# Joining the 32-wide inverse blocks of both head groups in one run on eight 32x32 tiles, with VectorE's block transpose for the transposed block

## The chip, the cores and the metric

The kernel runs on one core of one Trainium2 chip, as one program. Time is the device time of one launch in microseconds, and a kernel's time is the median of its runs. TensorE's matmuls, VectorE (DVE in the profile), ScalarE (ACT), GpSimd (POOL) and the DMA queues run side by side, each engine through its own list of instructions in order, and wait for each other by semaphores.

## The reference

A trunk of two layers over 256 tokens of width 1024. Each layer computes a gated DeltaNet branch in both directions and a differential attention branch from one input projection, gates and merges them, and projects out. The part that matters here is the DeltaNet's chunked form: in every chunk and head, and in both directions, a unit triangular matrix is inverted.

```python
    decay = jnp.where(lower, jnp.exp(jnp.where(lower, gdiff, 0.0)), 0.0)
    L = jnp.where(strict, jnp.einsum('bhncd,bhnmd->bhncm', kb, k) * decay, 0.0)
    eye = jnp.eye(CHUNK, dtype=f32)
    T = lax.linalg.triangular_solve(eye + L, jnp.broadcast_to(eye, L.shape),
                                    left_side=True, lower=True, unit_diagonal=True)
    u = jnp.einsum('bhncm,bhnme->bhnce', T, vb)
    w = jnp.einsum('bhncm,bhnmd->bhncd', T, kb * jnp.exp(g)[..., None])
```

Around it stand the large projections, `proj = h @ w_in[l]` (1024 x 10272), `y_a @ w_pa[l]`, `y_b @ w_pb[l]` and `merged @ w_out[l]`.

## The kernel before

**Projections.** Every projection of 512 columns is a stream of 128x512 products on TensorE. A weight block `kp` (256 rows, two of the eight `kt`) comes in by DMA as `raw`; ScalarE rounds it to `hi` (line 308), VectorE takes the rest as `lo` (line 310), and TensorE adds three products for each token tile `m`: input high by `hi` (line 324), input high by `lo` (line 325), input low by `hi` (line 326). So a block costs twelve 128x512 products, and those of line 325 can't start before VectorE has made `lo`. Buffers for `hi` and `lo` are two each. `gb` and `ga` are the two gate projections, each in two halves; the numbers in a name such as `lo_ga002` are layer, half and `kp`.

**The inverse.** Chunks of 128 tokens are used, two (`c`) for each of eight heads and two directions (`d`). Heads go in two groups `g` of four (`j4`). VectorE inverts the 32x32 diagonal blocks by substitution earlier in the layer. Then TensorE joins the blocks: 32 wide to 64 wide in `merges(g)`, 64 wide to 128 wide in `join()`, and `chunks(g)` uses the result. `U_` (`U` for a group) holds the inverses at 128 columns for each of 16 cases, `T64` the blocks in the other orientation at 64 columns, `A` the decayed products of the keys. To join two 32-blocks b0 and b1, the kernel makes

- `y64p` = A(b0, b1) by T64(b0), which ScalarE copies to `y64` (lines 926 and 930);
- `zt64` from `y64` and U(b1); ScalarE writes it negated as the off-diagonal block of `U` (lines 940 and 952);
- `z64`, the same block in the other orientation and for the pair `mm == d` alone; ScalarE writes it negated into `T64` (lines 945 and 955).

`srcdst(d, mm)` gives (0, 1) or (2, 3) for direction 0, and (1, 0) or (3, 2) for direction 1. An operand's 32-partition quarter sets the row of TensorE's 32x32 tile that a product uses, and the quarter of its result in PSUM sets the column. So a group's products stand on four tiles in `y64p` and `zt64` and on two in `z64`. `T64` and `U` then go into `y128p` and `zt128` of `join()` (line 966), 64x64 products of both groups on four 64x64 tiles, whose results ScalarE evicts (lines 973, 975 and 983).

**What sets the order.** The program is scheduled ahead of the run, and then fixed on every engine. `behind(x)` makes an instruction stand after instruction x; `place(n)` is the last product of the n-th `kt` in the list of projections `zb, za, gb, ga, pb` (eight `kt` a half, so 32 to 47 is `gb` and 48 to 63 is `ga`). `run(gen, at)` issues one step of a generator behind `place(at)`; the list `order` near line 1267 says which step goes where. `weigh_q` (line 830) multiplies a PSUM bank of key-query products `kq` (line 789) by the decays on VectorE. `gate_yb` has VectorE scale the attention output (line 1202) and turn it in 32x32 blocks (line 249); it is issued in the same stretch.

## Time and profile before

| | before |
|---|---|
| median of 3 runs | 747.26 us (746.84 to 748.62) |
| profiled execution, its own time | 746.91 us |
| its span, first to last instruction | 745.2 us |
| TensorE matmul busy | 736.4 us (99%) |
| VectorE, ScalarE, GpSimd busy | 585.9 (79%), 482.5 (65%), 141.8 us (19%) |
| mean granted TensorE clock | 0.999 |

The profile is of one execution. In its timeline a row gives a start in us from the span's start, the time until the last instruction of the row has ended, the engine, line, operation, output<-inputs, the tile of TensorE, the shape and a count; in brackets stands how long the engine had been idle before it, and what it had waited for. An fp32 product on TensorE shows as two matmul instructions, an fp32r one (the projections) as one. The end of a matmul is modelled, so the step between two starts says more than a duration.

### The profile page before, as it was taken

To read this page: it belongs to the slowest core of one execution; us is meant where nothing else is said; L and a number is where in the kernel's file an instruction comes from. 1 tells how busy PE (TensorE), PEld (TensorE's weight loads), DVE (VectorE), ACT (ScalarE), POOL (GpSimd) and SP (SyncE) were. 2 spreads that over 40 slices of the span, in tenths; PEclk is the share of its full clock that TensorE was granted. 3 is DMA by queue.
4 is the path that set the end of the run, shared out by engine and by line. 5 is a ranking of instruction groups with operands and counts; after the bars stand their busy time and mean duration, and the time that the engine had idled before them with its cause. 6 is when DMAs were issued, how large, how long until landed. Compare 5 with 4: busy or idle time off the path is not lost.

```text
span 745.2 us, 13923 instructions
## 1 busy us (share of the span) xinstructions
PE 736.4 (99%) x5176; PEld 638.4 (86%) x5176; DVE 585.9 (79%) x1109; ACT 482.5 (65%) x1024; POOL 141.8 (19%) x221
## 2 busy tenths in 40 slices
PE   9999999999999999999999999999999999999996
PEld 6999899987888889888889899889778888998885
DVE  8696898999986865578668779899999769638782
ACT  6757775567877586645456578565787758666552
POOL 6004111112022442100000150202110425301000
PEclk9999999999999999999999999999999999999999
DMA  8755566776766462567674466768666737336641
GB/s 260 240 171 171 169 172 195 216 204 205 209 182 173 148 193 89 171 203 241 204 233 130 131 194 177 214 175 237 200 170 198 199 120 233 106 119 203 216 142 58
DMA packets 73734, 135.46 MB, mean 182 GB/s; under 512 B 12944, under 2 KB 13921, under 8 KB 73666
## 3 DMA queue, kind: packets, MB, share of 16 engines
q1 hardware_dynamic: 64750, 113.65, 50.7%
q0 software_dynamic: 7936, 19.35, 9.1%
q10 hardware_dynamic: 980, 1.58, 0.6%
q8 instruction: 41, 0.67, 0.4%
q14 instruction: 27, 0.22, 0.1%
HBM read 125.53 MB, written 9.01 MB: 181 GB/s over the span
## 4 chain that ended last, share of the span: by engine, by line
PE 96%; ACT 2%; issue 1%; DVE 1%; POOLq 0%; POOL 0%; DVEq 0%; ACTq 0%
PE pp_vb L369 4%; PE pp_qk L325 4%; PE pp_qk L326 3%; PE pp_qk L324 3%; PE sc L1072 2%; PE pp_o L369 2%; PE pf_k L385 2%; PE pp_za L325 2%; PE pf_v L385 2%; PE pf_v L389 2%; PE pp_gb L325 2%; PE pp_gb L324 2%; PE pp_zb L324 2%; PE pf_q L387 2%; PE pf_k L387 2%; PE pf_v L387 2%
## 5 line engine op out<-in xcount | busy, mean ns | idle before, releaser
L325 PE MATMUL pp_qk<-lo_qk,hT 128*128 128x512 f32 x128 | 50.5, 395 | 0.3 <-DVE lo_qk L310 0.2
L326 PE MATMUL pp_qk<-hi_qk,hT 128*128 128x512 f32 x128 | 49.9, 390 | 0.0
L310 DVE TENSOR_TENSOR lo_qk<-raw_qk,hi_qk 128x1024 fp32r<-128x1024 f32 x32 | 39.0, 1220 | 9.8 <-ACT hi_qk L308 9.5
L324 PE MATMUL pp_qk<-hi_qk,hT 128*128 128x512 f32 x128 | 45.1, 393 | 0.0
L308 ACT CAST hi_qk<-raw_qk 128x1024 fp32r<-128x1024 f32 x28 | 29.4, 1050 | 23.4 <-PE pp_qk L326 12.7
L1082 ACT ACTIVATE es<-sc,mx 128x256 f32<-128x256 f32 x64 | 29.7, 475 | 19.6 <-DVE mx L1080 19.6
L310 DVE TENSOR_TENSOR lo_pb<-raw_pb,hi_pb 128x1024 fp32r<-128x1024 f32 x16 | 19.6, 1224 | 25.2 <-ACT hi_pb L308 25.2
L387 PE MATMUL pf_q<-hT,hi_q 128*128 128x256 f32 x128 | 36.1, 286 | 0.0
L385 PE MATMUL pf_k<-hT,hi_k 128*128 128x256 f32 x128 | 36.0, 287 | 0.0
L385 PE MATMUL pf_v<-hT,hi_v 128*128 128x256 f32 x128 | 35.9, 285 | 0.0
L387 PE MATMUL pf_v<-hT,hi_v 128*128 128x256 f32 x128 | 35.8, 284 | 0.0
L387 PE MATMUL pf_k<-hT,hi_k 128*128 128x256 f32 x128 | 35.7, 284 | 0.0
L385 PE MATMUL pf_q<-hT,hi_q 128*128 128x256 f32 x128 | 35.7, 284 | 0.0
L389 PE MATMUL pf_q<-hT,lo_q 128*128 128x256 f32 x128 | 35.2, 288 | 0.0
L389 PE MATMUL pf_v<-hT,lo_v 128*128 128x256 f32 x128 | 34.5, 288 | 0.0
L389 PE MATMUL pf_k<-hT,lo_k 128*128 128x256 f32 x128 | 34.3, 283 | 0.0
L308 ACT CAST hi_pa<-raw_pa 128x1024 fp32r<-128x1024 f32 x16 | 16.9, 1055 | 22.2 <-PE pp_pa L326 16.1
L679 DVE SCALAR_TENSOR_TENSOR cvq<-pf_q,cw,cvq 128x254 f32<-128x254 f32 (+1 forms) x64 | 29.9, 477 | 0.9 <-ACT cvq L675 0.2
L679 DVE SCALAR_TENSOR_TENSOR cvk<-pf_k,cw,cvk 128x254 f32<-128x254 f32 (+1 forms) x64 | 29.0, 477 | 1.4 <-ACT cvk L675 0.6
L325 PEld LDWEIGHTS pp_qk<-lo_qk,hT 128*128 128x128 f32 x128 | 24.0, 188 | 6.7 <-DVE lo_qk L310 1.7
L679 DVE SCALAR_TENSOR_TENSOR cvv<-pf_v,cw,cvv 128x254 f32<-128x254 f32 (+1 forms) x64 | 29.6, 472 | 0.1
L310 DVE TENSOR_TENSOR lo_pa<-raw_pa,hi_pa 128x1024 fp32r<-128x1024 f32 x16 | 19.6, 1223 | 11.2 <-ACT hi_pa L308 11.2
(415 smaller groups left out, 2537.9 us busy)
## 6 DMA issues: line engine op xcount, KB each, us to landing
raw_qk<-in_w_in_dram SPq DMA_DIRECT2D x32, 512.0 KB, 3.8
raw_k<-in_w_in_dram SPq DMA_DIRECT2D x16, 512.0 KB, 4.5
raw_q<-in_w_in_dram SPq DMA_DIRECT2D x16, 512.0 KB, 3.7
raw_v<-in_w_in_dram SPq DMA_DIRECT2D x16, 512.0 KB, 3.8
raw_zb<-in_w_in_dram SPq DMA_DIRECT2D x16, 512.0 KB, 3.9
raw_za<-in_w_in_dram SPq DMA_DIRECT2D x16, 512.0 KB, 3.7
raw_ga<-in_w_in_dram SPq DMA_DIRECT2D x16, 512.0 KB, 4.5
raw_pb<-in_w_pb_dram SPq DMA_DIRECT2D x16, 512.0 KB, 3.7
```

What stands on the lines that cost most here:

```text
L308: high = (V.tensor_copy if kp in turned else S.copy)(hi[:, :, :n], raw[:, :, :n]).ins
L310: mark[nm, kp] = high, V.tensor_tensor(lo[:, :, :n], raw[:, :, :n], hi[:, :, :n].bitcast(F32), ALU.subtract).ins
L324: T.matmul(o, act[kt // 4][:, 0, kt % 4, ts_], hi, start=kt == 0, stop=False)
L325: T.matmul(o, act[kt // 4][:, 0, kt % 4, ts_], lo, start=False, stop=False)
L326: mark["proj"] = T.matmul(o, act[kt // 4][:, 1, kt % 4, ts_], hi, start=False, stop=kt == KT - 1).ins
L369: mark["proj"] = T.matmul(o, act[kt // 4][:, pa, kt % 4, ts_], ws[kt][1 + pw], start=kt == 0 and n_ == 0, stop=kt == KT - 1 and n_ == 2).ins
L385: T.matmul(o, hi[:, cs], act[kt // 4][:, 0, kt % 4, :], start=first, stop=False, skip_group_check=True)
L387: T.matmul(o, hi[:, cs], act[kt // 4][:, 1, kt % 4, :], start=False, stop=False, skip_group_check=True)
L389: T.matmul(o, lo[:, cs], act[kt // 4][:, 0, kt % 4, :], start=False, stop=done, skip_group_check=True)
L679: V.scalar_tensor_tensor(ca[:, o0:o1], acc[:, b, o0 + sft : o1 + sft], cw[:, j, cb : cb + 1], ca[:, o0:o1], ALU.mult, ALU.add)
L1072: mm = T.matmul(sp[n][:, qt * SEQ : (qt + 1) * SEQ], qkT[h // 4][rows, 0, h % 4, qt * P : (qt + 1) * P], qkT[h // 4][rows, 1, h % 4, :], s ...
L1082: S.activation(es[:, n, qt, :], spv[:, qt, :], AF.Exp, bias=mx[:, n, qt : qt + 1], accum_out=s_all[:, h, n, qt : qt + 1])
```

## The change

The first step of the join (32 to 64 wide) moves from `merges(g)` into `join()` and is done for both groups at once. Group 1 writes its results to other quarters of PSUM (`across`: two quarters further), so its products stand on four further tiles: eight tiles in all. Results then lie in other partitions, and `y64` of group 1 is copied in two halves (two 64-partition copies in place of one of 128). `z64` and its two evictions for each group go; in their place VectorE turns the finished off-diagonal block of `U` into `T64` with four block transposes of 32 partitions by 8x32 elements. Four copies of negated `U` blocks that these need are issued first. In the table of places the steps move from 41, 43, 45, 48 and 50 to 41, 43, 47 and 49, and the last `weigh_q` from 47 to 46.

```diff
-            y64p = v4(bank_c(f"y64p{l}{g}")[:, :256])
-            y64 = work.tile([P, NM, 4, 32], F32, tag="w2c", name=f"y64{l}{g}", bufs=3)
-            order = [(c, j4, mm, d) for c, j4 in every for mm in range(2) for d in range(2)]
+            across = lambda b, g: (b + 2 * g) % 4
+            y64p = [v4(bank_c(f"y64p{l}{g}")[:, :256]) for g in range(2)]
+            y64 = [work.tile([P, NM, 4, 32], F32, tag="w2c", name=f"y64{l}{g}", bufs=3) for g in range(2)]
+            order = [(c, j4, s2, d, g) for c, j4 in every for g in range(2) for s2 in range(2) for d in range(2)]
...
-                    mm_ = T.matmul(y64p[blk(b1), c, j4, :], A[blk(b0), g, c, j4, blk(b1)],
-                                   T64[blk(b0), tix(d, c, j4), co : co + 32], start=True, stop=True)
+                    made = T.matmul(y64p[g][blk(across(b1, g)), c, j4, :], A[blk(b0), g, c, j4, blk(b1)],
+                                    parts[g][1][blk(b0), tix(d, c, j4), co : co + 32], start=True, stop=True)
...
-            S.copy(y64, y64p)
+            S.copy(y64[0], y64p[0])
+            for h_ in range(2):
+                S.copy(y64[1][halves[h_]], y64p[1][halves[1 - h_]])
             yield
...
             for c, j4 in every:
-                for mm in range(2):
-                    for d in range(2):
-                        b0, b1 = srcdst(d, mm)
-                        with behind(first):
-                            T.matmul(zt64[blk(b0), c, j4, :], y64[blk(b1), c, j4, :],
-                                     U[blk(b1), tix(d, c, j4), blk(b1)], start=True, stop=True)
-            for c, j4 in every:
-                for d in range(2):
-                    b0, b1 = srcdst(d, d)
-                    T.matmul(z64[blk(b1), c, j4, :], U[blk(b1), tix(d, c, j4), blk(b1)],
-                             y64[blk(b1), c, j4, :], start=True, stop=True)
-            for d in range(2):
-                td = slice(8 * d, 8 * d + 8)
-                fl = lambda z, b: z[blk(b)].rearrange("p c h i -> p (c h) i")
-                for mm in range(2):
-                    b0, b1 = srcdst(d, mm)
-                    S.mul(U[blk(b0), td, blk(b1)], fl(zt64, b0), -1.0)
-                b0, b1 = srcdst(d, d)
-                co = 32 * (b0 % 2)
-                S.mul(T64[blk(b1), td, co : co + 32], fl(z64, b1), -1.0)
+                for g in range(2):
+                    for s2 in range(2):
+                        for d in range(2):
+                            b0, b1 = srcdst(d, s2)
+                            with behind(mark["pin"]):
+                                T.matmul(zt64[g][blk(across(b0, g)), c, j4, :], y64[g][blk(b1), c, j4, :],
+                                         parts[g][0][blk(b1), tix(d, c, j4), blk(b1)], start=True, stop=True)
+            for own in (True, False):
+                for g in range(2):
+                    U, T64 = parts[g]
+                    for d in range(2):
+                        td = slice(8 * d, 8 * d + 8)
+                        b0, b1 = srcdst(d, d if own else 1 - d)
+                        S.mul(U[blk(b0), td, blk(b1)], fl(zt64[g], across(b0, g)), -1.0)
+                        if own:
+                            co = 32 * (b0 % 2)
+                            V.transpose(T64[blk(b1), td, co : co + 32], U[blk(b0), td, blk(b1)])
             yield
...
-                    lambda: [weigh_q(n // 2, n % 2, place((39, 42, 44, 47)[n])) for n in range(4)]),
+                    lambda: [weigh_q(n // 2, n % 2, place((39, 42, 44, 46)[n])) for n in range(4)]),
...
-        order = [(mg[:2], 41), (mg[:1], 43), (mg[1:2], 45), (mg[2:], 48), (mg[2:], 50)]
+        order = [(mg[2:], 41), (mg[2:], 43), (mg[2:], 47), (mg[2:], 49)]
```

How it moves instructions, at three places of layer 0 (layer 1 has the same ones). First TensorE in the second half of `gb`, at the third weight block, where the products `zt64` and `z64` of group 0 stood (`zt6400` and `z6400` in the rows, the last digit being the group) and group 1's followed seventeen rows later. Before:

```order
L325 MATMUL pp_gb010_2765<-lo_gb012_2802,hT0_1_127 128x512
L326 MATMUL pp_gb010_2765<-hi_gb012_2801,hT0_1_127 128x512
L940 MATMUL zt6400_3302<-U__96,y6400_3233 32x32 x32
L945 MATMUL z6400_3303<-y6400_3233,U__96 32x32 x16
L324 MATMUL pp_gb011_2766<-hi_gb012_2801,hT0_1_127 128x512
```

Now, in the same place, with rows of four for each group that alternate until each has 32:

```order
L324 MATMUL pp_gb010_2765<-hi_gb012_2801,hT0_1_127 128x512
L325 MATMUL pp_gb010_2765<-lo_gb012_2802,hT0_1_127 128x512
L945 MATMUL zt6400_3303<-U__96,y6400_3234 32x32 x4
L945 MATMUL zt6401_3304<-U__96,y6401_3235 32x32 x4
...
L326 MATMUL pp_gb010_2765<-hi_gb012_2801,hT0_1_127 128x512
```

Both groups' products stand here, those of the other orientation nowhere, and the second place is gone.

Second VectorE, from the end of `gb` into the first half of `ga`. `B0` is the weighing by `kq`, `lo_ga000` to `lo_ga002` are the low parts of the first three weight blocks of `ga`, `ktm0` a scaling of keys for the chunks, `ob` and `zb` the attention output and its turning, `tb_q` a turning of queries. Before:

```order
L249 STREAM_TRANSPOSE zb0_0_385<-ob0_0_383 128x4x4x32 x2
L830 TENSOR_TENSOR B0_371<-kq010_2849,B0_371 128x1024
L310 TENSOR_TENSOR lo_ga000_2899<-raw_ga000_2900,hi_ga000_2898 128x1024
...
L249 STREAM_TRANSPOSE zb0_1_386<-ob0_1_384 128x4x4x32
L830 TENSOR_TENSOR B0_371<-kq011_2855,B0_371 128x1024
L310 TENSOR_TENSOR lo_ga001_2917<-raw_ga001_2918,hi_ga001_2916 128x1024
...
L135 STREAM_TRANSPOSE tb_q00_3491<-kq0_359 128x512
L249 STREAM_TRANSPOSE zb0_1_386<-ob0_1_384 128x4x4x32
L310 TENSOR_TENSOR lo_ga002_2935<-raw_ga002_2936,hi_ga002_2934 128x1024
```

Now (a line that was 1202 is 1199, and 1009 is 1006):

```order
L249 STREAM_TRANSPOSE zb0_0_385<-ob0_0_383 128x4x4x32 x2
L956 STREAM_TRANSPOSE T6400_2654<-U__96 32x8x32 x2
L956 STREAM_TRANSPOSE T6401_2661<-U__96 32x8x32 x2
L830 TENSOR_TENSOR B0_371<-kq010_2849,B0_371 128x1024
L310 TENSOR_TENSOR lo_ga000_2899<-raw_ga000_2900,hi_ga000_2898 128x1024
...
L310 TENSOR_TENSOR lo_ga001_2917<-raw_ga001_2918,hi_ga001_2916 128x1024
L1006 TENSOR_TENSOR ktm0_360<-ktm0_360,kds0_372 128x512 x2
L249 STREAM_TRANSPOSE zb0_1_386<-ob0_1_384 128x4x4x32
L1199 SCALAR_TENSOR_TENSOR ob0_1_384<-ob0_1_384,rb0_2865,zb0_1_386 128x128 x4
L135 STREAM_TRANSPOSE tb_q00_3458<-kq0_359 128x512
L249 STREAM_TRANSPOSE zb0_1_386<-ob0_1_384 128x4x4x32
L310 TENSOR_TENSOR lo_ga002_2935<-raw_ga002_2936,hi_ga002_2934 128x1024
```

Four transposes are new ahead of the third `B0` weighing, and one turning of `zb` moves from ahead of `lo_ga001` to behind it; between the first row and `lo_ga002` stands otherwise the same set.

Third TensorE at the third weight block of the first half of `ga`. Before:

```order
L326 MATMUL pp_ga001_2897<-hi_ga001_2916,hT0_0_126 128x512
L966 MATMUL zt12800_3453<-U__96,y12800_3416 64x64 x8
L966 MATMUL zt12801_3454<-U__96,y12801_3417 64x64 x8
...
L324 MATMUL pp_ga000_2896<-hi_ga002_2934,hT0_1_127 128x512
L325 MATMUL pp_ga000_2896<-lo_ga002_2935,hT0_1_127 128x512
L326 MATMUL pp_ga000_2896<-hi_ga002_2934,hT0_1_127 128x512
```

Now:

```order
L326 MATMUL pp_ga001_2897<-hi_ga001_2916,hT0_0_126 128x512
L324 MATMUL pp_ga000_2896<-hi_ga002_2934,hT0_1_127 128x512
L324 MATMUL pp_ga001_2897<-hi_ga002_2934,hT0_1_127 128x512
L325 MATMUL pp_ga000_2896<-lo_ga002_2935,hT0_1_127 128x512
L326 MATMUL pp_ga000_2896<-hi_ga002_2934,hT0_1_127 128x512
```

The `zt128` products now stand ten 128x512 products further up, and one more product of line 324 stands ahead of the first that reads `lo_ga002`.

18 lines of the change are left out of this document (8 added, 10 removed).

## The prediction

> **What bounds the kernel now.** I read the page first, its busy times and the chain that ended last.
>
> ```profile
> PE 736.4 (99%) x5176; PEld 638.4 (86%) x5176; DVE 585.9 (79%) x1109; ACT 482.5 (65%) x1024; POOL 141.8 (19%) x221
> PE 96%; ACT 2%; issue 1%; DVE 1%; POOLq 0%; POOL 0%; DVEq 0%; ACTq 0%
> ```
>
> TensorE is the bound: 96% of the chain. A microsecond taken from its list is a microsecond gained, as long as what it reads is there in time. So I next read its timeline at the join in layer 0, to price the slots, and then the list of the engine that feeds it there.
>
> ```profile
> 239.78 0.39 PE L789 MATMUL kq<-kq 128*128 128x128 f32 x2
> 240.09 1.46 PE L926 MATMUL y64p<-T,A 32*32 32x32 f32 x128
> 241.49 0.50 PE L325 MATMUL pp_gb<-wgb,hT 128*128 128x512 f32 x1
> ...
> 245.03 0.39 PE L325 MATMUL pp_gb<-lo_gb,hT 128*128 128x512 f32 x1
> 245.26 0.40 PE L326 MATMUL pp_gb<-hi_gb,hT 128*128 128x512 f32 x1
> 245.59 0.72 PE L940 MATMUL zt<-U__96,y 32*32 32x32 f32 x62
> ...
> 246.17 0.65 PE L945 MATMUL z<-y,U__96 32*32 32x32 f32 x30
> 246.75 0.50 PE L324 MATMUL pp_gb<-hi_gb,hT 128*128 128x512 f32 x1
> ...
> 251.18 0.39 PE L324 MATMUL pp_gb<-hi_gb,hT 128*128 128x512 f32 x1
> 251.50 0.75 PE L940 MATMUL zt<-U__96,y 32*32 32x32 f32 x64
> 252.11 0.69 PE L945 MATMUL z<-y,U__96 32*32 32x32 f32 x32
> 252.73 0.50 PE L325 MATMUL pp_gb<-lo_gb,hT 128*128 128x512 f32 x1
> ...
> 257.26 1.16 PE L966 MATMUL y128p<-T,A 64*64 64x64 f32 x64
> ...
> 261.76 1.44 PE L966 MATMUL zt<-U__96,y 64*64 64x64 f32 x64
> 263.13 0.50 PE L324 MATMUL pp_ga<-hi_ga,hT 128*128 128x512 f32 x1
> 263.46 0.39 PE L325 MATMUL pp_ga<-lo_ga,hT 128*128 128x512 f32 x1
> ```
>
> A 128x512 product follows another after 0.23 us (245.03 to 245.26). Into a 32x32 slot it takes 0.33, and behind one the first product takes 0.33 as well (263.13 to 263.46, behind a 64x64 slot): some 0.1 on each side. The reader is to keep the last row: the first product that needs `lo_ga002`, at 263.46. This is VectorE's list up to that operand:
>
> ```profile
> 245.38 0.17 DVE L1244 SCALAR_TENSOR_TENSOR rb<-rb,r 128x16 f32<-128x16 f32 x1 [0.55 <-POOL rb L156]
> 245.59 2.19 DVE L1202 SCALAR_TENSOR_TENSOR ob<-ob,rb,zb 128x128 f32<-128x128 f32 x8
> 247.70 2.00 DVE L249 STREAM_TRANSPOSE zb<-ob 128x512 f32<-128x512 f32 x2
> 249.55 1.20 DVE L830 TENSOR_TENSOR B<-kq,B 128x1024 f32<-128x1024 f32 x1
> 251.10 1.23 DVE L310 TENSOR_TENSOR lo_ga<-raw_ga,hi_ga 128x1024 fp32r<-128x1024 f32 x1 [0.35 <-ACT hi_ga L308]
> 252.25 1.29 DVE L1009 TENSOR_TENSOR ktm<-ktm,kds 128x512 f32<-128x512 f32 x2
> 253.45 1.13 DVE L1202 SCALAR_TENSOR_TENSOR ob<-ob,rb,zb 128x128 f32<-128x128 f32 x4
> 254.62 1.13 DVE L249 STREAM_TRANSPOSE zb<-ob 128x512 f32<-128x512 f32 x1
> 255.60 1.20 DVE L830 TENSOR_TENSOR B<-kq,B 128x1024 f32<-128x1024 f32 x1
> 256.74 1.19 DVE L310 TENSOR_TENSOR lo_ga<-raw_ga,hi_ga 128x1024 fp32r<-128x1024 f32 x1
> ...
> 260.08 0.70 DVE L135 STREAM_TRANSPOSE tb_q<-kq 128x512 f32<-128x512 f32 x1
> 260.71 1.06 DVE L249 STREAM_TRANSPOSE zb<-ob 128x512 f32<-128x512 f32 x1
> 261.60 1.22 DVE L310 TENSOR_TENSOR lo_ga<-raw_ga,hi_ga 128x1024 fp32r<-128x1024 f32 x1
> ```
>
> From 245.38, where GpSimd's power lets it go, to 262.82 VectorE has no gap but 0.35 us. The three `lo_ga` rows are the first three weight blocks of `ga`; the third is ready at 261.60 + 1.22 = 262.82, and TensorE takes it at 263.46: **0.64 us of slack**. So VectorE's 79% is an average; in these 17 us it is as full as TensorE, and a gain on TensorE runs into it.
>
> **The change on TensorE.** Now the slots cost, with 0.09 ahead (245.49 to 245.59 and the like) and 0.10 behind: `y64p` 0.09 + 1.40 + 0.10 = 1.59; the first `zt`/`z` slot from 245.26 + 0.23 to 246.75 and 0.10 more, 1.36; the second from 251.41 to 252.73, 1.42. Together 4.37 us a layer.
>
> The new runs are two, of 128 instructions each on eight tiles. One instruction takes about 0.19 us from start to end:
>
> ```profile
> L945 PE MATMUL z<-y,U__96 x128: 184/191/212, 246.1 to 616.9; 32*32 32x32 f32 x128
> ```
>
> So starts in `z` lie (0.65 - 0.19) / 29 = 15.9 ns apart on two tiles, 32 ns for a tile's turn; in the second `zt` (0.75 - 0.19) / 63 = 8.9 ns on four tiles, 36 ns a turn; in `y64p` 1.27 / 127 = 10.0 ns, 40 ns. With twice the tiles the step halved while the turn hardly moved, so the tile's turn is the limit, not the issue. `y128p` has four tiles that share rows and columns in pairs, as the eight will, and takes some 15 ns a step, 60 ns a turn with twice the columns; nothing speaks of a loss by sharing. On eight tiles 128 instructions are 16 turns: 0.51 us at 32 ns, 0.64 at 40; I take 0.62. With 0.09 ahead, 0.12 from the last start to the next product (246.17 + 0.65 - 0.19 = 246.63, next at 246.75) and 0.10, a slot is 0.93, two 1.87: **2.50 us less a layer**. The bounds: 32 ns a turn gives 2.73; no closer step than now (10.0 and 8.9 ns) gives 1.27 + 1.13 + 0.62 = 3.02, so 1.35 saved. If nothing waited, two layers would gain 5.0 us, 2.7 to 5.5.
>
> **The change on ScalarE.** Four evictions of `z` go, `y64` has one copy more. Eight copies into `U` now stand in one row:
>
> ```profile
> 246.38 1.54 ACT L952 ACTIVATE U__96<-zt 32x256 f32<-32x256 f32 x4 [4.17 <-PE zt L940]
> 250.02 1.05 ACT L308 CAST hi_ga<-raw_ga 128x1024 fp32r<-128x1024 f32 x1 [1.31 <-PE pp_gb L326]
> ```
>
> The `zt` slot starts at 245.59 - 0.66 (the gain on `y64p`) - 0.23 (one product earlier) = 244.70 and ends near 245.5. At 0.385 each the four that the transposes need are done by 247.2, all eight by 248.7. The cast of `hi_ga000` waits for the last product of `gb`'s third block, which comes 1.1 us earlier (0.66 and the 0.43 of the first `zt` slot), so it ends near 250.0. Both are hidden: VectorE gets to the transposes at 249.55 and to `lo_ga000` after 252, and its old wait of 0.35 us is gone.
>
> **The change on VectorE.** Added are four transposes of 32 partitions by 256 elements ahead of `lo_ga002`; one turning of `zb` moves within the same stretch, which leaves `lo_ga002` where it was. No such transpose is in the trace. From below: half of the plain 512-element one's step (260.08 to 260.71), 0.32. From above: all of the strided one (254.62 to 255.60), 0.98. It is nearest to the plain one, which also reads and writes runs of 32 elements; the scalar-tensor rows take 0.26 for 128 elements (2.11 / 8) and the plain transpose 0.63 for 512, which puts 256 near 0.38. Four: 1.5 us (1.26 to 3.9). `lo_ga002` is then ready at 262.82 - 0.35 + 1.50 = 263.97. How soon TensorE goes on after such a wait is shown where it waited for a low part already:
>
> ```profile
> PE pp_qk L325 <- DVE lo_qk L310: 0.2, 1, 0.2
> 80.79 1.23 DVE L310 TENSOR_TENSOR lo_qk<-raw_qk,hi_qk 128x1024 fp32r<-128x1024 f32 x1
> 82.07 0.50 PE L325 MATMUL pp_qk<-lo_qk,hT 128*128 128x512 f32 x1
> ```
>
> 0.05 after the end. So the product starts at 264.02.
>
> **The sum.** Without a wait TensorE would come to it at 263.46 - 2.50 + 0.23 (one more product of line 324 stands ahead) = 261.19. It waits 2.8 us there, and all that was gained is gone: against the same work before (263.69) it is 0.33 us late. How well the eight tiles do doesn't matter, for even at 1.35 us saved it comes at 262.34. Ahead of that place, `y128p` waits for the transposes (done by 251.1; TensorE gets there at 257.26 - 2.50 less ten products, 252.5), and `lo_ga001` is ready at 257.93 - 0.35 + 1.50 - 0.98 = 258.1, just as TensorE comes to it, twelve products before 261.19; waits there would only take from the later one. Behind it VectorE is 1.2 us late, but TensorE then has a run of 128x128 chunk products to do before the fourth block, so nothing is late next, and TensorE is the bound again. Two cuts a layer in the runs of chunk products cost at most the 0.1 of a slot's side, 0.4 us in all; I take nothing, since the tile's size doesn't change there. Layer 1 has the same lists. So +0.66 us: the profiled execution's 746.91 becomes 747.6, and the median of 747.26, which lies 0.35 above it, **747.9 us**. With transposes at 0.32 it is +0.2, with free ones -2.3.
>
> **Rivals.**
>
> *The gain comes through.* VectorE would have to be 2.8 us earlier or `lo_ga002` wanted later. For it speaks that TensorE waits for almost nothing now; against it the gapless row of VectorE, whose start hangs on GpSimd. 746.91 - 5.0 = 741.9, with the median's offset 742.3.
>
> *Only a part is swallowed.* If VectorE's stretch were some 1.2 us shorter than read (transposes as good as free), 747.26 - 2.3 = 744.9.
>
> *The transposes are dear.* At the strided one's 0.98 each, whatever their size, VectorE is 2.4 us later still in each layer: 747.9 + 4.8 = 752.7. It is slower beyond the bound of 0.3% from 0.58 us each. Against it: the plain transpose has 0.63 for twice the elements.
>
> *The clock falls in the new gap.* TensorE idle for 2.8 us might lose its clock. At the end of the trace it does:
>
> ```profile
> 736.93 1.60 PE L359 MATMUL pp_o<-wB_o,mT 128*128 128x256 f32 x12
> 743.00:744.00 1.00, 0.00 (x0) 0.00 (x0) 0.00 (x0) 0.00 (x0) 0.00 (x0) 0.59 0.23 75
> ```
>
> TensorE ends at 738.53; a mean of 0.59 in the slice from 743, with 0.5 behind, puts the fall at 743.2, 4.65 us idle. Were it to happen in the gap and to last as long, half the clock would cost 2.3 us a layer: 752.5. The gap is shorter than the one seen, so the chance is small. The Trainium skill (TensorE: Matmul & The Clock Gate, Part 1) says that an idle window of about 3.4 us halves the clock until one as long has been busy; the trace agrees in the halving, and by this rule 2.8 us would not trip it, or if so cost 1.7 us a layer, 751.3.
>
> **How the numbers follow.** Swallowed whole, 747.9: 0.76. The gain through: 0.08. A part: 0.04. Dear transposes: 0.08. The clock: 0.04. A measurement of this kernel tells about 0.3%, 2.2 us, from no change. Faster: 0.12 (the two cases of a gain, the second being at the bound); slower: 0.12; within: 0.76. The likeliest case has 747.5 to 749 by its bounds; with the 1.8 us over which the runs before spread, and the case of a part, the range is 745.2 to 750.0.
>
> **What would show it.** Right: in the profile of the changed kernel the waits of TensorE name `lo_ga` of line 310 twice, near 2.8 us each, the 32x32 runs take near 0.8 us for 128 instructions, VectorE has no gap between the power's release and `lo_ga002`, and the span is within 2 us of 745.2. Wrong: no such wait and a span near 740; transposes over 0.58 us; a granted clock under 1 after the gap.

## The result and the profile after

| | before | after |
|---|---|---|
| median of 8 runs each | 747.06 us (746.73 to 748.62) | 749.78 us (748.69 to 752.51) |
| ratio, 95% interval | | 1.0038 (1.0024 to 1.0052) |
| profiled execution, its span | 746.91, 745.2 us | 751.0, 749.3 us |
| mean granted clock of the profiled execution | 0.999 | 0.996 |

The changed kernel is slower by 0.38%, with an interval on both sides of the 0.3% that I took as the limit of what can be told. 749.78 us lies inside the range given (745.2 to 750.0), 0.2 us under its upper end and 1.9 us above the forecast; "within", which I had given 0.76, is not what the medians say. The first reading of the new profile is TensorE's busy time on the page, and then its list of waits (total in us, times, longest).

```profile
PE 736.0 (98%) x5048; PEld 636.9 (85%) x5048; DVE 590.5 (79%) x1117; ACT 480.9 (64%) x1018; POOL 140.8 (19%) x221
```

```profile
PE pp_ga L325 <- DVE lo_ga L310: 4.1, 2, 2.1
```

128 matmul instructions are gone, and yet TensorE's busy time is hardly shorter (736.4 before). The waits named are those that were forecast, two of them at `lo_ga`, but of 2.1 us and not 2.8. Next TensorE's timeline in layer 0, at the two joined runs and at `lo_ga002`.

```profile
240.47 1.29 PE L930 MATMUL y64p<-T,A 32*32 32x32 f32 x128
...
245.25 0.39 PE L325 MATMUL pp_gb<-lo_gb,hT 128*128 128x512 f32 x1
245.57 1.29 PE L945 MATMUL zt<-U__96,y 32*32 32x32 f32 x128
246.78 0.50 PE L326 MATMUL pp_gb<-hi_gb,hT 128*128 128x512 f32 x1
...
264.77 0.50 PE L325 MATMUL pp_ga<-lo_ga,hT 128*128 128x512 f32 x1 [2.06 <-DVE lo_ga L310]
...
265.92 0.63 PE L324 MATMUL pp_ga<-hi_ga,hT 128*128 128x512 f32 x1
266.35 0.63 PE L325 MATMUL pp_ga<-lo_ga,hT 128*128 128x512 f32 x1
```

Two things stand here that my sum did not have. The runs of 128 instructions take 1.29 us each where I had forecast 0.8: (1.29 - 0.19) / 127 = 8.7 ns a step, no closer than the 8.9 that `zt` had on four tiles. And behind the wait a 128x512 product takes 0.43 us (265.92 to 266.35) and not 0.23. The windows on TensorE (start and end, length, busy time and instructions of PE, PEld, DVE, ACT and POOL, then the granted clock, the DMA share and GB/s) show why:

```profile
262.25:265.66 3.41, 1.35 (x7) 0.79 (x6) 3.41 (x4) 2.85 (x5) 1.19 (x3) 1.00 0.41 154
265.66:269.07 3.41, 3.41 (x11) 2.73 (x10) 3.41 (x6) 3.38 (x6) 2.20 (x5) 0.50 0.79 242
```

From 265.66 to 269.07 the clock is at half: 3.41 us, right behind a stretch of the same length in which TensorE was busy for 1.35 us, 40%. (The 1.7 us that half a clock costs there are most of why the busy time above is hardly shorter: in the last kernel below, with the same products and no such fall, it is 733.5.) VectorE's list up to `lo_ga002`:

```profile
245.84 0.17 DVE L1241 SCALAR_TENSOR_TENSOR rb<-rb,r 128x16 f32<-128x16 f32 x1 [0.79 <-POOL rb L156]
...
248.16 2.01 DVE L249 STREAM_TRANSPOSE zb<-ob 128x512 f32<-128x512 f32 x2
250.20 1.84 DVE L956 STREAM_TRANSPOSE T<-U__96 32x256 f32<-32x256 f32 x4
252.07 1.23 DVE L830 TENSOR_TENSOR B<-kq,B 128x1024 f32<-128x1024 f32 x1
...
263.52 1.20 DVE L310 TENSOR_TENSOR lo_ga<-raw_ga,hi_ga 128x1024 fp32r<-128x1024 f32 x1
```

It has no gap from 245.84 to 264.72, as forecast. The four transposes take 1.84 / 4 = 0.46 us each, and from the two turnings of `zb` to `B` it is now 252.07 - 248.16 = 3.91 us, where it was 249.55 - 247.70 = 1.85: 2.06 us more, and I had 1.5.

One measure carries the rest of this text: **the stretch**, from the first `y64p` product to the first product of `pp_pb`. It holds the same work in both kernels but for the change, and leaves out how the program starts. Rows of before, and then of after, one pair for each layer (of a pair whose first row stands above, only the second):

```profile
297.48 0.47 PE L324 MATMUL pp_pb<-hi_pb,ybT 128*128 128x512 f32 x1
604.41 1.47 PE L926 MATMUL y64p<-T,A 32*32 32x32 f32 x128
661.80 0.47 PE L324 MATMUL pp_pb<-hi_pb,ybT 128*128 128x512 f32 x1
```

```profile
300.32 0.47 PE L324 MATMUL pp_pb<-hi_pb,ybT 128*128 128x512 f32 x1
607.72 0.97 PE L930 MATMUL y64p<-T,A 32*32 32x32 f32 x91
665.88 0.47 PE L324 MATMUL pp_pb<-hi_pb,ybT 128*128 128x512 f32 x1
```

Before it is 57.39 us in both layers (297.48 - 240.09; 661.80 - 604.41). After it is 59.85 in layer 0, where the clock fell, and 58.16 in layer 1, where the wait was 2.01 us and the clock stayed at 1.00. So a layer lost 0.77 us by the wait, and one fall of the clock cost 59.85 - 58.16 = 1.69 us more.

The eight executions can be read by this. Their mean granted clocks are 0.999 three times (748.69 to 748.95 us), 0.996 four times (749.7 to 751.0) and 0.994 once (752.51). One fall takes 0.5 x 3.41 / 749 = 0.0023 off the mean. The fall at the program's end takes off more or less as well, since it begins 2.0 us ahead of the last instruction in the profile of before and 4.6 us ahead in another: the nine full profiles of this study with no other fall read 0.997 to 0.999, the two with one read 0.996. So I read the eight as no fall, one and two: six falls at 16 waits. Only one of these executions was traced. Without a fall the sum is 747.06 + 2 x 0.77 = 748.6, which is what those three show.

### The profile page after: what moved, and what is told of

The parts are those of the page before. It is cut to its first block, busy times and chain, and to the rows that moved or that the text cites. A ratio compares the mean times of both kernels' runs of the same rounds, so it can differ in the third digit from the quotient of the medians.

```text
span 749.3 us, 13675 instructions
## 1 busy us (share of the span) xinstructions
PE 736.0 (98%) x5048; PEld 636.9 (85%) x5048; DVE 590.5 (79%) x1117; ACT 480.9 (64%) x1018; POOL 140.8 (19%) x221
## 5 line engine op out<-in xcount | busy, mean ns | idle before, releaser
L325 PE MATMUL pp_ga<-lo_ga,hT 128*128 128x512 f32 x64 | 26.2, 410 | 4.1 <-DVE lo_ga L310 4.1
```

What stands on the lines that cost most here:

```text
L325: T.matmul(o, act[kt // 4][:, 0, kt % 4, ts_], lo, start=False, stop=False)
```

## The experiments

The theory at this point: VectorE's lateness at `lo_ga002` eats all that TensorE gains; TensorE gains some 1.3 us a layer and not 2.5, since eight tiles step no faster than four; and the wait lets the clock fall in some executions. In the table the stretch is that of the profiled execution, the layers apart; the results follow one by one.

| kernel | us, median | ratio to before | stretch, us |
|---|---|---|---|
| before | 747.0 to 747.1 | | 57.39, 57.39 |
| changed | 749.78 | 1.0038 (1.0024 to 1.0052) | 59.85, 58.16 |
| low part first | 745.84 | 0.9987 (0.9978 to 0.9996) | 56.78, 56.67 |
| the same on four tiles | 746.0 | 0.9983 (0.9974 to 0.9992) | 56.68, 56.73 |
| gap filled | 749.53 | 1.0036 (1.0023 to 1.005) | 58.18, 58.43 |
| before, low part first | 747.3 | 1.0014 (1.0002 to 1.0026) | 57.44, 57.43 |
| longer wait | 753.84 | 1.0089 (1.0077 to 1.0101) | 60.70, 59.05 |
| products for the transposes | 753.12 | 1.0085 (1.0071 to 1.0099) | 60.62, 58.80 |
| products in a place of their own | 747.05 | 1.0003 (0.9994 to 1.0012) | 58.17, 58.74 |
| queries' turning behind too | 747.91 | 1.0016 (1.0007 to 1.0024) | 57.82, 57.61 |
| list cleared | 744.53 | 0.9970 (0.9961 to 0.9979) | 56.14, 56.11 |

### The low part first

```diff
-            at = [mark[f"ga{l}0", m][1] if i else mark[f"gb{l}1", 2 + m][1] for m in range(NM)]
+            at = [mark[f"ga{l}0", 1 + m][1] if i else mark[f"gb{l}1", 2 + m][1] for m in range(NM)]
```

> The changed kernel, but the last scalings and turnings of the attention output (four scalings of line 1199, 1.06 us, and one turning of line 249, 1.05 us) stand behind lo_ga002 on VectorE instead of ahead of it; nothing is left out. Theory (the gain on TensorE is eaten by VectorE's lateness at lo_ga002): lo_ga002 is ready 2.1 us earlier, when TensorE comes to it; the waits of 2.06 and 2.01 us and the fall of the clock behind them go: 748.8 (the changed kernel without a fall) - 4.1 = 744.7 us, between 744.0 and 745.4; granted clock 0.999. Rival 1 (what stood ahead of lo_ga002 is missed behind it: a wait of TensorE for another low part or for ybT takes the place): 746.5 to 749. Rival 2 (the eight tiles saved the 2.50 us a layer that I predicted, and the trace misleads): 742.3 us.

Measured: 745.84 us (745.07 to 746.88), 1.1 us above the number expected and outside its range, but on its side: faster than before, by 0.13%. The granted clock is 0.997 in nine of the eleven executions and not 0.999; in the profile, with 0.997, it falls at the program's end alone. The list of waits of this kernel says what is missing, and its row of `lo_ga002` why.

```profile
PE pp_ga L325 <- DVE lo_ga L310: 1.4, 2, 0.7
```

```profile
261.33 1.22 DVE L310 TENSOR_TENSOR lo_ga<-raw_ga,hi_ga 128x1024 fp32r<-128x1024 f32 x1
```

0.7 us of the wait is left in each layer. Counted from `y64p` (240.16 in this profile), `lo_ga002` is ready at 262.55 - 240.16 = 22.4 us where the changed kernel had 24.25, so 1.9 us earlier and not 2.1; and TensorE, whose products stand in another order too, comes to it 0.5 us earlier than there. The stretch is 0.6 and 0.7 us below before's; with the 0.7 still waited for, the joined run is worth some 1.3 to 1.4 us a layer. No other wait has come: the first rival falls, and so does the second, with its 742.3.

### The joined run on four tiles

```diff
-            across = lambda b, g: (b + 2 * g) % 4
+            across = lambda b, g: b
...
-                S.copy(y64[1][halves[h_]], y64p[1][halves[1 - h_]])
+                S.copy(y64[1][halves[h_]], y64p[1][halves[h_]])
```

> The kernel with the low part first, with both groups still joined in one run, but on four 32x32 tiles instead of eight (group 1 writes to the same quarters of PSUM as group 0, in a bank of its own); the instructions and their order are the same; nothing is left out. Theory (the issue of products is the limit, about 16.5 ns a product of two matmuls, however many tiles): the runs of 128 take about as long, 8.9 to 10.0 ns a step in place of 8.6, so 0.05 to 0.2 us a run, and the time is that of eight tiles + 0.2 to 0.8 us: 745.2 us. Rival (the tile's turn is the limit, 66 ns when eight share rows and columns, and four tiles have a turn of 36): the same step on four, so the time is the same within 0.3 us, 744.7; if four tiles should need twice the step (17 ns), each run would be 1.1 us longer and the time 749.

Measured: 746.0 us against 745.84, and a stretch of 56.68 and 56.73 against 56.78 and 56.67. The runs of 128 take 1.33 and 1.29 us here. The eight tiles are worth nothing; the two theories are told apart by the next kernel and not by this one. What the change saves on TensorE is `z64` and a slot.

### Tiles by themselves

One of the sixteen runs, that on four tiles with 32 columns; the others differ in the list of tiles (row, column), the columns and the count.

```diff
+    for r, c in list(((0, 1), (1, 0), (2, 3), (3, 2))) * 16:
+        tc.keep_in_program_order(T.matmul(four[(c - r) % 4][q(c), :32], ones[q(r), q(c)], ones[q(r), :32], start=True, stop=True))
+    pause()
```

> The kernel before with sixteen runs of fp32 products put ahead of it on constants, each of 64 products (128 matmul instructions; one of 640 instructions), with a pause of wide products between them; the total time says nothing. In order: 32 columns on two, four, eight, sixteen tiles and one; 64 columns on four, eight, sixteen; 128 columns on one, on four in different rows and columns, on four in one row, on four in one column, on eight, on sixteen; the 640 on four with 32 columns; four with 32 again. Theory (issue is the limit, about 8.3 ns an instruction): 32 columns take 8.3 to 9 ns a step on four, eight and sixteen tiles, 16 on two, 32 on one; 64 columns 15 on four and 8 to 9 on eight and sixteen; 128 columns about 28 on four, 14 on eight, 8 to 9 on sixteen. Rival (tiles that share a row or a column do not run side by side): eight and sixteen tiles take as long as four at every width (8.5, 15, 28), and the four in one row or one column up to four times 28. The 640: if the feed of instructions gives out as in the run of 192 (2.2 us), one gap or more of about 2 us.

The timeline, one row for each run of 128 instructions. In order: two, four, eight, sixteen tiles with 32 columns; four and eight with 64; with 128 columns four in different rows and columns, four in one row, four in one column, eight, sixteen; and the first two rows of the run of 640.

```profile
10.40 2.21 PE L419 MATMUL tl<-ones 32*32 32x32 f32 x128
17.89 1.29 PE L422 MATMUL tl<-ones 32*32 32x32 f32 x128
24.45 1.29 PE L425 MATMUL tl<-ones 32*32 32x32 f32 x128
31.02 1.29 PE L428 MATMUL tl<-ones 32*32 32x32 f32 x128
...
50.34 1.99 PE L434 MATMUL tl<-ones 32*32 32x64 f32 x128
57.61 1.47 PE L437 MATMUL tl<-ones 32*32 32x64 f32 x128
...
102.21 3.70 PE L446 MATMUL tl<-ones 32*32 32x128 f32 x128
111.18 3.70 PE L449 MATMUL tl<-ones 32*32 32x128 f32 x128
120.15 3.70 PE L452 MATMUL tl<-ones 32*32 32x128 f32 x128
129.13 2.02 PE L455 MATMUL tl<-ones 32*32 32x128 f32 x128
136.43 1.90 PE L458 MATMUL tl<-ones 32*32 32x128 f32 x128
143.61 1.55 PE L461 MATMUL tl<-ones 32*32 32x32 f32 x161
147.05 1.93 PE L461 MATMUL tl<-ones 32*32 32x32 f32 x128 [1.89 <-issue]
```

With the 0.19, 0.21 and 0.27 us off that one instruction takes with 32, 64 and 128 columns, and 127 steps in what is left, a step is 15.9 ns on two tiles and 8.7 on four, eight and sixteen with 32 columns; 14.0 on four and 9.9 on eight with 64 (and 10.0 on sixteen, whose row took 1.48 us); 27.0 on four, 13.8 on eight and 12.8 on sixteen with 128. So tiles that share rows and columns do run side by side (27.0 to 13.8, and four in one row or one column take no longer than four apart), and the rival falls. But there is a floor on the step that tiles don't move: 8.7 ns with 32 columns, and four tiles stand on it already. With 128 columns sixteen tiles are hardly better than eight, so the floor rises with the columns; 8 to 9 ns for sixteen, with 64 as with 128 columns, was expected and is wrong. Why it rises, these runs don't tell.

The last two rows are a second limit. A run of more than some 160 small instructions stops: after the first 161 a gap of 1.89 us named "issue", and then one of 1.5 to 1.8 us after every 128. (From 146.86 on the granted clock is at half, so the second row and what follows show that clock; the first gap began ahead of it.)

### The gap filled

```diff
...
-                T.matmul(o, act[kt // 4][:, 0, kt % 4, ts_], hi, start=kt == 0, stop=False)
+                high = T.matmul(o, act[kt // 4][:, 0, kt % 4, ts_], hi, start=kt == 0, stop=False).ins
+                for _ in range(9 if nm in ("ga00", "ga10") and (kt, m) == (4, 1) else 0):
+                    with behind(high), tc.high_priority(offset=HP): high = T.matmul(fill, act[1][:, 0, 0, ts_], hi, start=True, stop=True).ins
```

> The changed kernel with nine idle 128x512 products of line 324's kind, 0.23 us each, put into TensorE's list ahead of the first product that reads lo_ga002, in both layers; their result is not used; nothing is left out. They fill the gap of 2.06 us with work. Theory (the clock falls because TensorE idles in the gap): no fall in any execution, granted clock 0.999 or more in all, and the time is that of the changed kernel without a fall: 748.8 us, 748.3 to 749.4, with a spread under 1 us. Rival (the clock falls for another reason, the load of the chip or the 32x32 runs): executions of 750 to 752 stay among them, the median near 749.8.

Measured: 749.53 us, 748.47 to 750.58. The granted clock is 0.997 or 0.998 in all five executions, against 0.996 and less in five of the eight of the changed kernel, and in the traced one it is 1.00 through the place of the gap: no fall where TensorE has work. The stretch, 58.18 and 58.43, is near that of the changed kernel without a fall (58.16). That far the theory holds. But the spread is 2.1 us, not under 1, and the median is 0.7 us above the 748.8 expected; by its times alone the result is the rival's (749.8, with executions above 750), and it is the clock that speaks against it. So the falls are not the whole of the spread. Part of the rest lies at the program's start: the first product of line 464 stands at 9.29 us here and between 8.35 and 10.50 in the profiles of this study, with nothing changed ahead of it. The two latest, 10.50 and 10.46, are the profiles of the products for the transposes and of the queries' turning; there the six matmul instructions of line 452 a little ahead of it take 1.65 us, and 0.94 in the others. So a profiled execution can be 1.7 us longer than before's (8.76) by its start alone. Whether the untraced executions differ by this I can't say.

### Before, with the low part first

The edit is that of the first experiment, in the kernel before.

> The kernel before with the same move of the last scalings and turnings behind lo_ga002, without the joined run; nothing is left out. Theory (the joined run saves 1.3 us of TensorE in a layer and the wait alone eats it): the kernel before has no wait there, so the move is worth nothing: 747.1 us, 746.6 to 747.6. Rival (the move is a gain by itself, and the joined run adds nothing): 746.0 us, as with the low part first in the changed kernel.

Measured: 747.3 us, ratio 1.0014 (1.0002 to 1.0026); the stretch is 57.44 and 57.43. The move by itself brings nothing, so the gain above is the joined run's. Two executions of 750.7 and 751.5 us stand apart from the other ten. The second has a granted clock of 0.996, as with one fall, the first 0.999; they were not traced, and I can't say what they are.

### A longer wait

```diff
-        V.transpose(tb.rearrange("p j (d k) -> p j k d", k=4), src.rearrange("p k (j t) -> p j k t", j=4))
+        for _ in range(1 + (nm in ("yb010", "yb110"))): V.transpose(tb.rearrange("p j (d k) -> p j k d", k=4), src.rearrange("p k (j t) -> p j k t", j=4))
```

> The changed kernel with one turning of the attention output (line 249, 0.95 to 1.05 us) done twice just ahead of lo_ga002, in both layers; the result is the same; nothing is left out. VectorE's lateness: each wait becomes 3.0 us, +2.0 us: 750.8 us where the clock does not fall. The clock, theory (TensorE's idle share is judged in windows of 3.41 us on a fixed grid, and 2.0 us idle in one halves the clock in the next): a wait of 3.0 us holds 2.0 in one window in (3.41 + 3.0 - 2 x 2.0) / 3.41 = 0.7 of the positions, so 1.4 falls an execution, 1.7 us each: median 753.2 us, granted clock 0.996 or less in most. Rival (the length of the wait does not matter for the fall, as often as now, 6 in 16 waits): median 752.0 us, a third of the executions without a fall.

Measured: 753.84 us (752.31 to 755.18), 0.6 above the theory's 753.2 and 1.8 above the rival's. The granted clock is 0.996 twice and 0.994 three times: by the reading above 2 x 1 + 3 x 2 = 8 falls at 10 waits, where the windows gave 0.7 and the rival 0.4. The profiled execution had one of its two waits with a fall (2.94 us, layer 0) and one without (2.88 us, layer 1):

```profile
262.84:266.25 3.41, 0.72 (x3) 0.63 (x4) 3.41 (x4) 3.31 (x6) 1.12 (x2) 1.00 0.32 121
266.25:269.66 3.41, 3.41 (x14) 3.02 (x13) 3.41 (x6) 3.41 (x6) 2.20 (x4) 0.50 0.83 250
...
631.48:634.90 3.42, 1.62 (x10) 1.44 (x11) 3.42 (x5) 3.35 (x6) 1.57 (x3) 1.00 0.58 164
634.90:638.31 3.41, 3.41 (x27) 3.15 (x26) 3.41 (x5) 3.41 (x7) 3.41 (x8) 1.00 0.70 239
```

On the grid that the fall in layer 0 sets (every 3.413 us from it), the wait in layer 1 is cut in two by a boundary at 631.48; the window behind the boundary is 1.62 / 3.42 = 47% busy, and the clock stays. So a window at 40% (the changed kernel) halves the next, one at 47% doesn't, and a wait of about 2 us trips it only where it falls nearly whole into one. By this, (3.41 - 2.06) / 3.41 = 0.40 of the places on the grid are such, an estimate; the 6 of 16 read above are 0.38. In layer 1 of the changed kernel the wait was cut in the same way, into windows of 73% and 68%. The program's end in the profile of the joined run on four tiles adds a point: this window, 42% busy, was followed by half a clock.

```profile
736.33:739.74 3.41, 1.43 (x12) 1.23 (x11) 1.10 (x5) 0.62 (x3) 0.56 (x1) 1.00 0.36 132
```

The grid is shown in the changed kernel's own end as well: the clock fell at 746.93, 477.86 us behind the end of the first fall, which is 140 windows of 3.413.

```profile
746.93:749.30 2.37, 0.00 (x0) 0.00 (x0) 0.00 (x0) 0.00 (x0) 0.00 (x0) 0.50 0.18 58
```

The Trainium skill (TensorE: Matmul & The Clock Gate, Part 1) calls the window free-running and 3413 ns long; the runs agree in the length and in that it does not start with a wait. It has the clock fall after a window that is idle; here one that was busy for 40% was enough.

### Products in place of the transposes

```diff
...
+            for c, j4 in every:
+                for g in range(2):
+                    for d in range(2):
+                        b0, b1 = srcdst(d, d)
+                        with behind(mark["pin"]):
+                            T.matmul(z64[g][blk(across(b0, g)), c, j4, :], parts[g][0][blk(b1), tix(d, c, j4), blk(b1)],
+                                     y64[g][blk(b1), c, j4, :], start=True, stop=True)
...
-                            V.transpose(T64[blk(b1), td, co : co + 32], U[blk(b0), td, blk(b1)])
+                            S.mul(T64[blk(b1), td, co : co + 32], fl(z64[g], across(b0, g)), -1.0)
```

> The changed kernel on its eight tiles, but the block of T64 made by products again (32 more products, 64 matmul instructions, on four tiles behind the zt64 run; ScalarE evicts them), and no VectorE transposes; the order is otherwise the same; nothing is left out. Theory (the four transposes, 2.06 us of VectorE's list, make lo_ga002 late): the wait at lo_ga002 is gone, TensorE has 64 instructions more at about 9 ns, 0.55 to 0.6 us a layer: 748.8 - 4.1 + 1.1 = 745.8 us, 745.2 to 746.5, clock 0.999. Rival (the run on eight tiles itself costs, not the transposes): a wait or a longer run stays and the time is not under 747.1.

Measured: 753.12 us, the slowest but for the longer wait; the expectation missed by 7 us. TensorE's timeline and ScalarE's, in layer 0, show two things that I had left out:

```profile
247.96 0.37 PE L954 MATMUL zt<-y,U__96 32*32 32x32 f32 x21
250.51 0.56 PE L954 MATMUL zt<-y,U__96 32*32 32x32 f32 x41 [2.17 <-issue]
251.07 0.37 ACT L962 ACTIVATE U__96<-zt 32x256 f32<-32x256 f32 x1 [6.90 <-PE zt L954]
...
255.74 1.05 ACT L308 CAST hi_ga<-raw_ga 128x1024 fp32r<-128x1024 f32 x1
```

The run is now 192 instructions long, and it stops for 2.17 us after some 150: the limit that the run of 640 shows. In layer 1 it stops for 0.43 us only, after some 130. And ScalarE's copies wait for the whole run, and then twelve stand in a row, so the cast of `hi_ga000` begins at 255.74 where the changed kernel had it at 250.29. VectorE and then TensorE get it late, and TensorE still waits 1.5 us at `lo_ga002`. Nor are these two the whole of the 6 us over before: the profiled execution starts 1.7 us late, as told above, and the other three have granted clocks of 0.995, 0.992 and 0.994 against its 0.998, which by the reading above is one fall or two in each. So this kernel doesn't tell what the transposes cost; it tells that products in this place are dear.

### Products in a place of their own

```diff
...
                         S.mul(U[blk(b0), td, blk(b1)], fl(zt64[g], across(b0, g)), -1.0)
-                        if own:
...
+            yield
+            for c, j4 in every:
...
+                            T.matmul(z64[g][blk(across(b0, g)), c, j4, :], parts[g][0][blk(b1), tix(d, c, j4), blk(b1)],
+                                     y64[g][blk(b1), c, j4, :], start=True, stop=True)
...
+                    S.mul(parts[g][1][blk(b1), 8 * d : 8 * d + 8, co : co + 32], fl(z64[g], across(b0, g)), -1.0)
             yield
...
-        order = [(mg[2:], 41), (mg[2:], 43), (mg[2:], 47), (mg[2:], 49)]
+        order = [(mg[2:], 41), (mg[2:], 43), (mg[2:], 45), (mg[2:], 47), (mg[2:], 49)]
```

> The joined run on eight tiles with T64's block by products and no VectorE transposes, but the 32 products in a place of their own, some ten wide products behind zt64, so that no run is longer than 128 instructions, and U's copies ahead of T64's on ScalarE; nothing is left out. Theory (in the products' first trial two things other than the transposes cost time: a run of 192 small instructions outruns the feed, 2.2 and 0.4 us, and twelve evictions in a row make the cast of hi_ga000 late): no gap by issue in the run, no wait at lo_ga002, TensorE has 0.75 us more a layer than in the changed kernel without its waits: 744.6 + 1.5 = 746.1 us, 745.5 to 746.9. Rival (products cost more on TensorE than that, or T64 comes late to y128p): 747 or more, with a wait at y128p or y1p.

Measured: 747.05 us, no change against before. It is the rival's number (747 or more), though not its wait. The 6 us of the last kernel are gone and so is the wait at `lo_ga`. Both causes named there were taken away at once, so their shares are not shown; that no wait is left at `lo_ga` without the transposes agrees with their making it late. But the products cost more than the 0.75 us a layer that I had for them. The profiled execution, with 748.64 us the longest of its eleven, waits 0.5 us a layer at the `qs` products for VectorE's `vtm`, and in layer 1 it has a gap of 0.51 us named "issue" one wide product behind the run of 128, where none was expected. What the rest of the 0.9 us is, I leave open.

### The queries' turning behind `lo_ga002` too

```diff
-                with behind(mark["weighed"]):
+                with behind(mark[f"ga{l}0", 2][1]):
                     turn_squares(
```

(on top of the low part first)

> The kernel with the low part first, and the first turning of the queries (line 135, 0.63 us) behind lo_ga002 too; nothing is left out. Theory (what is left of the wait, 0.7 us in each layer, is VectorE's list still): lo_ga002 is ready 0.63 us earlier, the wait falls to about 0.1: 746.0 - 1.2 = 744.8 us, 744.2 to 745.4. Rival (another wait takes its place, for the turnings or for a low part behind): 745.7 or more.

Measured: 747.91 us, 2.1 us slower than without it; the rival was right. TensorE's and ScalarE's rows:

```profile
267.07 3.84 PE L994 MATMUL y1p<-vtm,U__96 128*128 128x128 f32 x32 [0.75 <-ACT U__96 L980]
265.17 0.63 ACT L1048 ACTIVATE tb_q<-tb_q 128x512 f32<-128x512 f32 x1 [3.86 <-DVE tb_q L135]
265.83 2.43 ACT L980 ACTIVATE U__96<-zt 64x512 f32<-64x512 f32 x4
```

ScalarE squares the turned queries (line 1048) ahead of its copies into `U` (line 980). Turned later, they hold ScalarE for 3.86 us with nothing to do, `U` comes late, and the chunk products wait for it. Of the wait at `lo_ga002` 0.18 us is left; the rest did not end, it moved to the next operand in another engine's list. That is a part of the 1.0 us by which a layer's stretch is longer than with the low part first: counted from `y64p`, the chunk products begin 25.43 us behind it and not 25.07, 0.36 later. The other 0.7 us are lost behind that, and what takes them the list of waits doesn't name.

### The list cleared

```diff
-                with behind(mark["weighed"]):
+                with behind(mark[f"ga{l}0", 2][1] if h else mark["weighed"]):
                     turn_squares(tb, kq[:, h : h + 2, :, 1, :].rearrange("p h m t -> p (h m) t"))
-                S.activation(tb, tb, AF.Square)
-                V.tensor_reduce(qpart[:, :, h : h + 2, :].rearrange("p j h m -> p j (h m)"), tb,
-                                AX.X, ALU.add)
+                with behind(mark[f"ga{l}0", 2][0]):
+                    S.activation(tb, tb, AF.Square)
+                with behind(mark[f"ga{l}0", 2][1]):
+                    V.tensor_reduce(qpart[:, :, h : h + 2, :].rearrange("p j h m -> p j (h m)"), tb, AX.X, ALU.add)
...
-            at = [mark[f"ga{l}0", 1 + m][1] if i else mark[f"gb{l}1", 2 + m][1] for m in range(NM)]
+            at = [mark[f"ga{l}0", 2][1] if i else mark[f"gb{l}1", 2 + m][1] for m in range(NM)]
```

(on top of the low part first)

> The changed kernel with VectorE's list ahead of lo_ga002 cleared of all that TensorE does not wait for: both lots of scalings and turnings of the attention output and the later turnings and sums of the queries stand behind it, while the first turning of the queries stays ahead and ScalarE squares it where it did, so that ScalarE does not stall ahead of U's eviction; nothing is left out. Theory (the joined run saves 1.3 us of TensorE in a layer, and all of it shows once no operand is late): lo_ga002 is ready 1.5 us earlier than with the last lot alone behind it, TensorE waits for nothing there: 746.0 - 1.4 = 744.6 us, 744.0 to 745.3. Rival (the list is only as long as it is: what was put behind lo_ga002 makes lo_ga003 or U's eviction late by as much): 745.8 or more, with a wait at another product.

Measured: 744.53 us (743.76 to 746.96), ratio 0.9970 (0.9961 to 0.9979), as expected and faster than both kernels. The page's busy times, the wait, VectorE's row of `lo_ga002` in the timeline, and TensorE's row in layer 0 that waits:

```profile
PE 733.5 (99%) x5048; PEld 634.8 (85%) x5048; DVE 590.1 (79%) x1117; ACT 480.3 (65%) x1018; POOL 141.8 (19%) x221
```

```profile
PE pp_ga L325 <- DVE lo_ga L310: 0.4, 2, 0.2
```

```profile
258.75 1.18 DVE L310 TENSOR_TENSOR lo_ga<-raw_ga,hi_ga 128x1024 fp32r<-128x1024 f32 x1
268.54 0.50 PE L325 MATMUL pp_ga<-lo_ga,hT 128*128 128x512 f32 x1 [0.20 <-DVE lo_ga L310]
```

VectorE does as much as in the changed kernel (590.1 us), only in another order. `lo_ga002` is ready at 258.75 + 1.18 = 259.93, and TensorE, which comes to it at 260.48, doesn't wait. What is left is 0.2 us a layer at the next low part, `lo_ga003` (268.54): a little of what was put behind `lo_ga002` is missed there, as the rival has it, but little. The stretch is 56.14 and 56.11, some 1.27 us under before's, and twice that, 2.5 us, is the difference of the medians. All but these 0.2 us a layer of what TensorE gains shows once nothing stands ahead of `lo_ga002` that could stand behind. The same clearing in the kernel before was not run; that kernel's list of waits names none at `lo_ga`, so I would expect nothing of it.

## Why the prediction was right and where it was wrong

- **"All that was gained is gone" at `lo_ga002`.** Right, and the main thing. VectorE was gapless, the wait came at the row named, twice, of 2.06 and 2.01 us. Taking work from ahead of `lo_ga002` turned 749.8 us into 745.8 and 744.5 without a change to the join.
- **"The tile's turn is the limit, not the issue."** Wrong. I read 36 to 40 ns a turn on four tiles as the tile's own time, from the step of 15.9 ns on two; on four the floor of 8.7 ns holds, whatever the tiles, and the two readings give nearly the same number there. A slot became 246.78 - (245.25 + 0.23) + 0.10 = 1.40 us and not 0.93, and the gain some 1.45 us a layer (57.39 - 56.1, with 0.2 still waited for) and not 2.50. My lower bound of 1.35, made from the old steps, was nearly it. It didn't matter to the forecast, as its sum said: with less gained TensorE only waits less, 2.06 us and not 2.8.
- **"0.38" for a transpose of 32 partitions by 256 elements.** Mis-sized: 0.46, and 2.06 us for the four with their neighbours and not 1.5. I had put it on a line between two other operations, the 0.26 of a scalar-tensor row of 128 elements and the 0.63 of the plain turning of 512; why it doesn't lie there, the runs don't tell. Taken from `rb`, `lo_ga002` is ready after 264.72 - 245.84 = 18.88 us where I had 263.97 - 245.38 = 18.59.
- **"+0.33 us" a layer.** It was 0.77. From `y64p` to the first product with `lo_ga002` it is 264.77 - 240.47 = 24.30 us, where I had 264.02 - 240.09 = 23.93: 0.37 more. Of it 0.29 came on VectorE's list (the transposes 0.56 more, the rest of the list 0.27 less), and 0.08 because `rb` came later behind `y64p`. That is most of the 0.44; the 0.07 left is behind that place, and whether it is the two more cuts a layer, taken at nothing, is not shown.
- **"The clock falls in the new gap", 0.04.** The step that failed most. I held a wait of 2.8 us too short beside the 4.65 us of idle time at the program's end. But what counts is a window on a grid; at the end, too, it was one window of idle time that tripped it, and where the grid lay made 4.65 us of it. It fell in 6 of 16 waits, as read from the mean clocks, 1.7 us each and not 2.3. On the means of the eight executions of each kernel, 747.20 + 2 x 0.77 + 6 / 8 x 1.69 = 750.0, and 750.04 was measured.
- **"Nothing is late next"** behind `lo_ga002`. Right in the changed kernel; in the kernel with the queries' turning moved, the next operand was late at once.
- **ScalarE's part.** Right: its eight copies and the cast of `hi_ga000` stay hidden, though they end at 250.00 and 251.35 where I had 248.7 and 250.0; VectorE comes to `lo_ga000` at 253.21.

```profile
246.83 3.17 ACT L953 ACTIVATE U__96<-zt 32x256 f32<-32x256 f32 x8 [3.95 <-PE zt L945]
250.29 1.06 ACT L308 CAST hi_ga<-raw_ga 128x1024 fp32r<-128x1024 f32 x1 [0.29 <-PE pp_gb L326]
```

So the place and the direction were forecast, and the number came out within the range because two errors of size (less gained, dearer transposes) worked on a wait that takes up the first of them; what lifted the median by the last microsecond was the rival that I had all but left out. That it stayed inside is in part luck: three of the eight executions lie above 750.0, all of them read as having a fall. Of my own signs, the wait named twice and the gapless row came; the 0.8 us for a run and the span within 2 us of 745.2 did not, and a granted clock under 1 after the gap, which I had listed as a sign of being wrong, did.

## What to carry to other kernels

Where work is moved from the bound engine to a full one, look at what stands ahead of the operand that the bound engine takes next, and put what nobody waits for behind it; the gain shows only then (here 2.5 us faster than before in place of 2.7 slower). Then follow the moved work into the other lists, since an in-order engine that now waits for it holds everything behind it. And price a wait of TensorE of about 2 us or more with its chance of a fall of the clock, here 1.7 us, in 6 of 16 waits of 2.0 us and 8 of 10 of 2.9 (read from mean clocks).

## What the runs showed of the hardware that I had not expected

- A wait of 2.0 us in TensorE's list can halve its clock for 3.41 us, and whether it does depends on where it lies on a grid of 3.413 us (with wide products a window 40 or 42% busy trips it, one of 47% doesn't).
- Busy is not all that counts for it. In the run on one 32x32 tile TensorE had no idle time, and the clock fell in the next window:

```profile
37.64:41.05 3.41, 3.41 (x110) 3.41 (x110) 0.00 (x0) 0.00 (x0) 0.00 (x0) 1.00 0.02 5
41.05:44.46 3.41, 3.41 (x28) 2.24 (x25) 0.00 (x0) 0.00 (x0) 0.00 (x0) 0.50 0.02 5
...
102.48:105.90 3.42, 3.42 (x129) 3.22 (x117) 0.00 (x0) 0.00 (x0) 0.00 (x0) 1.00 0.02 5
105.90:109.31 3.41, 3.41 (x9) 1.56 (x9) 0.00 (x0) 0.00 (x0) 0.00 (x0) 1.00 0.00 0
```

  Four tiles with 128 columns for a whole window (the lower two rows) kept it. And in the run of 640 on four tiles a window 50% busy (143.45 to 146.86) was followed by half a clock, so the bounds above don't hold for small products. One tile gives 3.41 / 110 = 31 ns a step, four 8.7, so tiling is worth a factor of 3.6 with 32 columns, and more tiles add nothing. With 128 columns it is worth more: one tile did 34 instructions in a window at full clock (71.77 to 75.18), 100 ns a step, and sixteen take 12.8. The Trainium skill (TensorEngine Tiling (Array Packing), Overview) has up to 16 times for products that are small both ways, as a theoretical limit; here the floor on the step ends it at four tiles with 32 columns, and at a factor of 7.8 with 128.
- TensorE can't be fed small instructions for long at that step: after some 130 to 160 in a row it stopped for 0.4 to 2.2 us. Runs of 128 stay just inside in every profile but one, where 0.51 us were lost one wide product behind such a run.
